# Short-sequence attention on one core: transposes straight from the landed tiles, v by four rows a partition

## The chip, the cores and the metric

One core of a Trainium2 chip. The metric is the device time of one execution in microseconds (us). Every run lists a span (first to last instruction) and the clock that TensorE was granted. The profile is one execution; the times come from several, and the span of a profiled run is about 1.8 us shorter than its time. Executions fall into a fast and a slow state (the changed kernel: 139.7 to 140.9 us fast, 142.3 us slow). The medians below are of all runs of a kernel, the ratios of its fast runs alone; where it matters, the fast runs are named.

Engines: PE is TensorE (PEld its weight loads), DVE is VectorE, ACT is ScalarE, POOL is GpSimd, SP is SyncE. "The DMA" is the core's 16 DMA engines; the profile's page gives its shares of the time of all 16. In quoted lines "<-" names what ended a wait: a tile that another engine wrote or freed, a landing (DMA), PE's own sequencer (PEq), or "issue" where the profile shows nothing that was waited for.

## The reference

```python
batch, n_heads, seq, head_dim = 32, 12, 128, 64          # q, k, v: f32, 12.6 MB each
scores = 1 / np.sqrt(64) * np.matmul(q, k.transpose(0, 1, 3, 2))
attn = np.exp(scores - np.max(scores, axis=-1, keepdims=True))
attn = attn / (np.sum(attn, axis=-1, keepdims=True) + 1e-8)
return np.matmul(attn, v)
```

There are 384 heads. 37.75 MB are read and 12.58 MB written; the arithmetic is small.

## The kernel before

The heads go in 48 units of 8, and four units make a super-tile. A slab is a piece of q, k, v or the output with so many consecutive rows in each of the 128 partitions. POOL loads q, k and v and casts them from f32 to bf16 on the way (37.75 MB read from HBM, 18.87 MB landed by the packet sizes of the trace). q and k land with 16 consecutive rows of a head in one partition. DVE pairs rows of two slabs (128 values side by side), PE transposes the pairs with an identity, DVE empties the transposes' one PSUM bank, and scores, exponential, values and normalisation follow. v's keys are brought into the same order by matmuls with a selection matrix.

```python
NQ, NVB, NVE, NP, NT, NA = 4, 2, 8, 4, 2, 4      # buffers: q and k each, v, ordered v, pairs, ...
q_b = [sb(f"q_b{i}", [128, 2, 16 * D], bf16) for i in range(NQ)]
v_b = [sb(f"v_b{i}", [128, 4, RV * D], bf16) for i in range(NVB)]      # RV = 8 rows a partition
...
def pair_up(t):                                    # DVE
    src = (q_b, k_b)[j][s % NQ][:].rearrange("p a (r d) -> p r a d", d=D)
    return nc.vector.tensor_copy(pair[t_index[t] % NP][:], src[:, 8 * b:8 * b + 8])
...
for u in steps:                                    # one step a unit; the order of every engine's list
    for t in t_at.get(u, []): pe_transposes(t)     # waits for the pair and for the bank being empty
    for m in v_at.get(u, []): pe_order_v(m); act_keep(m)
    pe_scores(u + 1); act_exps(u + 1); pe_values(u); dve_normalise(u - 1)
    for t in t_at.get(u, []): dve_keep(t)          # empties the bank
    for t in t_at.get(u + 2, []): dve_pair(t)      # two steps AHEAD of the transposes
...
# POOL's loads: q and k wait for the pairs made of the buffer's last tile,
# v waits for the order matmuls of the group two before
deps = [("P", t) for t in t_order if t[0] == x - NQ and t[1] == j]
deps = [("V", sum(vgroups[:x - NVB + 1]) - 1)]
```

PE's list is a loop over 8 steps (two super-tiles). Its instructions name fixed buffers, so of what PE reads for a super-tile there are no more than two buffers here, one for each super-tile of the loop. The pairing copies are unrolled on DVE; that is why q and k could have four.

The softmax here doesn't subtract the row's maximum and nothing guards it: scores larger than these inputs give would overflow.

Of the kernel before, what the change touches and what calls it, by code (L numbers as in the profile page):

```python
# [10 lines left out]
def kernel(  # L11
# [7 lines left out]
    nc = tc.nc  # L19
# [13 lines left out]
    RO, SO = 4, S // 4  # L33
    RV, SV = 8, S // 8
    supers, u0 = [], 0
# [10 lines left out]
    k_rows = {R: slabs(k, R) for R in (16,)}  # L46
    v_rows, o_rows = slabs(v, RV), slabs(out, RO)

# [9 lines left out]
    vgroups = [4] * (NU // 4)  # L58
    stores = [1, 1] + [2] * ((NU - 4) // 2) + [1, 1]
    assert sum(vgroups) == NU and sum(stores) == NU  # L60
# [17 lines left out]
    for m in range(NU):  # L78
        v_at[m - 3] = [m]
    steps = range(min(t_at) - 2, NU + 1)  # L80

    NQ, NVB, NVE, NP, NT, NA = 4, 2, 8, 4, 2, 4

# [13 lines left out]
    ident = sb("ident", [128, 128], bf16)  # L97
    sel = {R: sb(f"sel{R}", [128, 8, 2, 32], bf16) for R in (16,)}
    q_b = [sb(f"q_b{i}", [128, 2, 16 * D], bf16) for i in range(NQ)]
    k_b = [sb(f"k_b{i}", [128, 2, 16 * D], bf16) for i in range(NQ)]  # L100
    v_b = [sb(f"v_b{i}", [128, 4, RV * D], bf16) for i in range(NVB)]
    v_e = [sb(f"v_e{i}", [128, 8, D + 1], bf16) for i in range(NVE)]
    pair = [sb(f"pair{i}", [128, 8, 2, D], bf16) for i in range(NP)]
    qkT = [sb(f"qkT{i}", [128, 2, 16, S], bf16) for i in range(NT)]
# [64 lines left out]
    def transposes(t):  # L169

        s, j, b = t
        R = supers[s][0]
        x = pair[t_index[t] % NP]
        p = qk_ps[:].rearrange("p (h r j s) -> p h r j s", h=R, r=4, j=2)
        for r in range(8):
            jj, r4 = divmod(r, 4)
            i = nc.tensor.transpose(  # L177
                p[:, :, r4, jj, :], x[:, r].rearrange("p a d -> p (a d)"), ident[:])
        return i

    def order_v(m):


        g, w, n, first = vplace[m]
        pick = sel[supers[of_unit[first]][0]]
        nh = 8 // n
        t = v_ps[:].rearrange("p (i n e) -> p i n e", i=nh, e=D)
        for i in range(nh):
            for jv in range(2):
                for r4 in range(4):  # L190
                    x = nc.tensor.matmul(  # L191
                        t[r4 * 32:(r4 + 1) * 32, i, :, :],
                        lhsT=pick[:, w * nh + i, jv, :],
                        rhs=v_b[g % NVB][:, :n, (4 * jv + r4) * D:(4 * jv + r4 + 1) * D],
                        start=jv == 0, stop=jv == 1)
        return x

    def v_at_head(u, a, h):

        R, f = supers[of_unit[u]]  # L200
        g, _, n, first = vplace[u]
        n8, h8 = divmod(a * R + 4 * (u - f) + h, 8)
        if n == 2:
            n8 = a
        nh = 8 // n
        return first + h8 // nh, (h8 % nh) * n + n8

# [30 lines left out]
    def exps(u):  # L238
# [5 lines left out]
            func=EXP, bias=0.0, scale=scale)  # L244

    def pair_up(t):

        s, j, b = t
        src = (q_b, k_b)[j][s % NQ][:].rearrange("p a (r d) -> p r a d", d=D)
        return nc.vector.tensor_copy(pair[t_index[t] % NP][:], src[:, 8 * b:8 * b + 8])  # L250

# [40 lines left out]
    def pe_transposes(t):  # L292
        i = t_index[t]
        deps = [("P", t)] + ([("E", t_order[i - 1])] if i else [])
        op("PE", ("T", t), lambda: transposes(t), deps, ["pe_dve"])

    def pe_wait(kind, key):
# [34 lines left out]

    def dve_pair(t):
        s, j, b = t
        deps = [("T", t_order[t_index[t] - NP])] if t_index[t] >= NP else []
        dma = [((s_q, s_k)[j][s % NQ], 16 * (s // NQ + 1))]
        op("DVE", ("P", t), lambda: pair_up(t), deps, ["dve_io"] if t_index[t] else ["dve_pe", "dve_io"], dma)

    def dve_keep(t):
        s = t[0]  # L340
        deps = [("T", t)]
        for x in range(s):
            if x % NT == s % NT:
                R, f = supers[x]
                deps.append(("S", f + R // 4 - 1))
        op("DVE", ("E", t), lambda: keep_qk(t), deps, ["dve_pe"])

# [23 lines left out]
    def store(c):  # L371
# [17 lines left out]
        last = first + n - 1  # L389
        op(name, ("store", c), emit, [("N", last if c in own else max(last, HELD))])  # L390

    def pool_load(kind, x):
        deps = []
        if kind == "v":
            if x >= NVB:
                deps = [("V", sum(vgroups[:x - NVB + 1]) - 1)]
            n, first = vgroups[x], sum(vgroups[:x])
            op("POOL", ("load", kind, x), lambda: nc.gpsimd.dma_start(  # L398
                out=v_b[x % NVB][:, :n, :], in_=v_rows[:, first:first + n, :],
            ).then_inc(s_v[x % NVB], 16), deps)  # L400
            return
# [3 lines left out]
        if x >= NQ:  # L405
            deps = [("P", t) for t in t_order if t[0] == x - NQ and t[1] == j]
        n = f * 8 // R
# [6 lines left out]


    op("ACT", ("K", -1), lambda: nc.scalar.drain(), [], ["act_pe"], v_landing(0))
    at_step = {}
    for u in steps:
# [20 lines left out]
        for t in t_at.get(u, []):  # L439
            dve_keep(t)  # L440
        for t in t_at.get(u + 2, []):
            dve_pair(t)
        for o in program["PE"][start:]:
# [3 lines left out]
    for s in range(len(supers)):  # L447
        for j in range(2):
            loads.append((t_step[s, j, 0] - 2, "qk"[j], s))
    for g in range(len(vgroups)):  # L450
        m = sum(vgroups[:g])

        loads.append((vstep_of[m] - 1.5 + (2 if 2 <= g < len(vgroups) - 2 else 0), "v", g))
    loads.sort(key=lambda e: e[0])
# [9 lines left out]
    seen = {e: {} for e in program}  # L464
    waited_dma = {e: {} for e in program}

# [31 lines left out]
    def tensor_program():  # L498
# [11 lines left out]
        for place in [(l, kind) for l in range(PERIOD) for kind in "TVSOQ"]:  # L510
# [4 lines left out]
            skipped = 0 if trips[0] else TRIPS - 1  # L515
            if waiting or not places or places[-1][0] != skipped or place == (1, "T"):
                places.append((skipped, waits[place] if waiting else [], []))
# [5 lines left out]
        with nc.Fori(  # L523
                0, TRIPS, engines=bass.OrderedEngineSet([nc.tensor.engine]),
                head_slot={nc.tensor.engine: 128}):
            for skipped, always, some in places:
                run_waits("PE", always)
                with nc.tensor.If_ne(trip, skipped):
                    for o, w in some:
                        run("PE", o, w)  # L530
            nc.tensor.reg_add(trip, trip, 1)
# [19 lines left out]

    for t in sel.values():
        nc.vector.memset(t[:], 0.0)
    nc.vector.memset(ident[:], 0.0).then_inc(s_zero, 1)
# [3 lines left out]

    for jv in range(2):
        nc.vector.tensor_copy(  # L560
            sel[16][:].rearrange("p h v (x y s) -> p h v x y s", x=2, y=2)[:, :, jv, :, jv, :],
            ident[:].rearrange("p (h s x) -> p h x s", h=8, x=2))
    for o in program["DVE"]:
# [38 lines left out]
```

## Time and profile before

| | |
|---|---|
| time | 134.2 us, median of 3 (132.2 to 134.65); 133.8 with the fourth run |
| span of the profiled run | 131.9 us |
| DMA | full from the second slice of 40 to the third from the end |
| DVE, PE, ACT busy | 69%, 74%, 56% |

The DMA row is the only one that is full nearly everywhere. The lines and their reading stand in the prediction.

### The profile page before, as it was taken

To read this page: it belongs to the slowest core of one execution; us is meant where nothing else is said; L and a number is where in the kernel's file an instruction comes from. 1 tells how busy PE (TensorE), PEld (TensorE's weight loads), DVE (VectorE), ACT (ScalarE), POOL (GpSimd) and SP (SyncE) were. 2 spreads that over 40 slices of the span, in tenths; PEclk is the share of its full clock that TensorE was granted. 3 is DMA by queue.
4 is the path that set the end of the run, shared out by engine and by line. 5 is a ranking of instruction groups with operands and counts; after the bars stand their busy time and mean duration, and the time that the engine had idled before them with its cause. 6 is when DMAs were issued, how large, how long until landed. Compare 5 with 4: busy or idle time off the path is not lost. (4 is left out here: it accounts for less than half of the span.)

```text
span 131.9 us, 7079 instructions
## 1 busy us (share of the span) xinstructions
PE 97.0 (74%) x3072; PEld 68.9 (52%) x3072; DVE 90.8 (69%) x214; ACT 73.7 (56%) x97; POOL 55.5 (42%) x81
## 2 busy tenths in 40 slices
PE   0014989994989999869849839978669998877610
PEld 0013647672667677656627626656456766555410
DVE  1126366895588999969939848969826988875740
ACT  0000528845577778476367366498084868588700
POOL 5950005015008259194460391390680399930000
PEclk9999999999599999999999999999986999999955
DMA  2999999999999999999999999999999999999982
GB/s 15 164 206 210 208 208 213 209 207 212 204 213 165 167 222 237 209 327 251 208 318 259 209 279 217 212 353 220 212 348 225 211 342 270 400 380 368 319 289 82
DMA packets 18248, 31.56 MB, mean 239 GB/s; under 512 B 1344, under 2 KB 9536, under 8 KB 18240
## 3 DMA queue, kind: packets, MB, share of 16 engines
q0 software_dynamic: 16064, 29.36, 101.3%
q1 hardware_dynamic: 2176, 2.10, 4.7%
q8 instruction: 4, 0.07, 0.2%
q14 instruction: 4, 0.03, 0.1%
HBM read 37.75 MB, written 12.58 MB: 381 GB/s over the span
## 5 line engine op out<-in xcount | busy, mean ns | idle before, releaser
L241 ACT ACTIVATE attnT<-s_ps 128x1024 bf16<-128x1024 f32 x48 | 49.4, 1030 | 0.4 <-PE s_ps L217 0.4
L236 ACT CAST v_e<-v_ps 128x512 bf16<-128x512 f32 x48 | 28.2, 588 | 37.0 <-PE v_ps L191 19.1
L177 PE MATMUL qk_ps<-ident,pair 128*128 128x128 bf16 x384 | 32.2, 232 | 15.3 <-PEq L478 15.1
L191 PE MATMUL v_ps<-v_b,sel 128*32 128x256 bf16 x768 | 31.9, 289 | 11.3 <-PEq L478 11.2
L272 DVE TENSOR_TENSOR o_sb<-o_ps,recip 128x512 f32<-128x512 f32 (+1 forms) x53 | 34.0, 641 | 4.8
L259 DVE COPY qkT<-qk_ps 128x1024 bf16<-128x1024 bf16 x48 | 32.8, 684 | 5.3 <-PE qk_ps L177 4.3
L177 PEld LDWEIGHTS qk_ps<-ident,pair 128*128 128x128 bf16 x384 | 24.2, 103 | 20.4 <-issue 17.9
L398 POOL DMA_DIRECT2D v_b<-in_v_dram x12 | 9.5, 791 | 59.7 <-PE v_ps L191 59.7
L387 POOL DMA_DIRECT2D out_dram<-o_sb x38 | 27.2, 729 | 0.0
L191 PEld LDWEIGHTS v_ps<-v_b,sel 128*32 128x32 bf16 x768 | 16.9, 99 | 17.8 <-issue 13.6
L228 PE MATMUL o_ps<-v_e,attnT 128*32 128x65 bf16 x1536 | 22.6, 200 | 1.7 <-PEq L478 0.8
L269 DVE RECIPROCAL recip<-o_ps 128x8 f32<-128x8 f32 (+1 forms) x53 | 10.5, 198 | 16.8 <-PE o_ps L228 16.0
L228 PEld LDWEIGHTS o_ps<-v_e,attnT 128*32 128x32 bf16 x1536 | 16.7, 98 | 7.5 <-issue 3.8
L217 PE MATMUL s_ps<-qkT 64*128 64x128 bf16 x384 | 19.5, 222 | 0.7 <-PEq L478 0.6
L217 PEld LDWEIGHTS s_ps<-qkT 64*128 64x128 bf16 x384 | 11.1, 95 | 11.3 <-issue 11.3
L250 DVE COPY pair<-q_b 128x1024 bf16<-128x1024 bf16 x24 | 11.1, 460 | 6.3 <-DMA q_b<-in_q_dram 6.2
L250 DVE COPY pair<-k_b 128x1024 bf16<-128x1024 bf16 x24 | 10.2, 427 | 0.0
L410 POOL DMA_DIRECT2D q_b<-in_q_dram x12 | 9.0, 747 | 1.0 <-SPq L96 1.0
L236 ACT ACT_TABLE_LOAD x1 | 1.3, 1283 | 13.7 <-DMA v_b<-in_v_dram 13.7
L410 POOL DMA_DIRECT2D k_b<-in_k_dram x12 | 8.6, 721 | 0.0
L560 DVE COPY sel<-ident 128x128 bf16<-128x128 bf16 x2 | 0.4, 224 | 1.8 <-POOL ident L537 1.8
L384 POOL DMA_DIRECT2D out_dram<-o_sb x2 | 1.5, 734 | 0.0
(8 smaller groups left out, 1.4 us busy)
## 6 DMA issues: line engine op xcount, KB each, us to landing
out_dram<-o_sb POOLq DMA_DIRECT2D x40, 256.0 KB, 10.2
q_b<-in_q_dram POOLq DMA_DIRECT2D x12, 512.0 KB, 13.2
k_b<-in_k_dram POOLq DMA_DIRECT2D x12, 512.0 KB, 12.7
v_b<-in_v_dram POOLq DMA_DIRECT2D x12, 512.0 KB, 10.2
out_dram<-o_sb SPq DMA_DIRECT2D x8, 256.0 KB, 4.3
```

The source lines that it names most:

```text
L177: i = nc.tensor.transpose(p[:, :, r4, jj, :], x[:, r].rearrange("p a d -> p (a d)"), ident[:])
L191: x = nc.tensor.matmul(t[r4 * 32:(r4 + 1) * 32, i, :, :], lhsT=pick[:, w * nh + i, jv, :], rhs=v_b[g % NVB][:, :n, (4 * jv + r4) * D:(4 * ...
L217: i = nc.tensor.matmul(t[:, a, h, :], lhsT=x[p, 1, 4 * w + h, :], rhs=x[p, 0, 4 * w + h, :], start=True, stop=True)
L228: y = nc.tensor.matmul(t[h * SO:(h + 1) * SO, a, r * (D + 1):(r + 1) * (D + 1)], lhsT=x[:, a, h, r * SO:(r + 1) * SO], rhs=v_e[m % NVE][:, ...
L236: return nc.scalar.copy(v_e[m % NVE][:, :, :D], v_ps[:].rearrange("p (n e) -> p n e", e=D))
L241: return nc.scalar.activation(out=attnT[u % NA][:].rearrange("p a h (r s j) -> p (a h r) s j", r=4, j=J), in_=s_ps[u % 2][:].rearrange("p ...
L250: return nc.vector.tensor_copy(pair[t_index[t] % NP][:], src[:, 8 * b:8 * b + 8])
L259: return nc.vector.tensor_copy(x.rearrange("p h (r j s) -> p (h r) j s", r=4, j=J)[:, :, 2 * b:2 * b + 2, :].rearrange("p x j s -> p x (j ...
L269: nc.vector.reciprocal(r, o4[:, :, :, D]).then_inc(s_r, 1)
L272: return nc.vector.tensor_mul(o[:, :, w, :].rearrange("p a (r d) -> p a r d", d=D), o4[:, :, :, :D], r.unsqueeze(3).to_broadcast([128, o4. ...
L387: e.dma_start(out=dst[:, a], in_=src[:, a]).then_inc(s_o[lane(c)], 16)
L410: nc.gpsimd.dma_start(out=bufs[x % NQ][:], in_=rows[R][:, n:n + 2, :]).then_inc(sm[x % NQ], 16)
```

## The change

Its intent is to drop 21 us of DVE copies and a third of the order matmuls' busy time on PE. Transposes read the landed q and k tiles, two of 64 columns where there was one of 128. v lands with 4 rows in a partition, eight slabs a group, so that one selection matrix of 32 columns puts its keys in order with 4 matmuls of 512 columns. q and k have two buffers, since PE reads them itself now. The kernel gives PE no wait for a transfer in its loop, so DVE waits for the next landing before it empties the bank.

```diff
-    v_rows, o_rows = slabs(v, RV), slabs(out, RO)
+    v_rows, o_rows = slabs(v, RO), slabs(out, RO)
-    stores = [1, 1] + [2] * ((NU - 4) // 2) + [1, 1]
+    stores = [1, 1] + [2] * ((NU - 8) // 2) + [1] * 6
-        v_at[m - 3] = [m]
+        v_at[m - 4] = [m]
-    NQ, NVB, NVE, NP, NT, NA = 4, 2, 8, 4, 2, 4
+    NQ, NVB, NVE, NT, NA = 2, 2, 8, 2, 4
 ...
-        x = pair[t_index[t] % NP]
+        x = (q_b, k_b)[j][s % NQ][:].rearrange("p a (r d) -> p r a d", d=D)[:, 8 * b:8 * b + 8]
         for r in range(8):
             jj, r4 = divmod(r, 4)
-            i = nc.tensor.transpose(
-                p[:, :, r4, jj, :], x[:, r].rearrange("p a d -> p (a d)"), ident[:])
+            for a in range(2):
+                i = nc.tensor.transpose(
+                    p[a * D:(a + 1) * D, :, r4, jj, :], x[:, r, a], ident[:])
 ...
-        for i in range(nh):
-            for jv in range(2):
-                for r4 in range(4):
-                    ...  # 16 matmuls of 256 columns, two accumulating
+        for r4 in range(4):
+            x = nc.tensor.matmul(
+                t[r4 * 32:(r4 + 1) * 32], lhsT=sel[:, w, :],
+                rhs=v_b[g % NVB][:, :, r4 * D:(r4 + 1) * D], start=True, stop=True)
 ...
-        op("DVE", ("E", t), lambda: keep_qk(t), deps, ["dve_pe"])
+        op("DVE", ("E", t), lambda: keep_qk(t), deps, ["dve_pe"], qk_landing(t_index[t] + 1))
 ...
-            deps = [("P", t) for t in t_order if t[0] == x - NQ and t[1] == j]
+            deps = [("T", t) for t in t_order if t[0] == x - NQ and t[1] == j]
 ...
-        for t in t_at.get(u + 2, []):
-            dve_pair(t)
 ...
-            loads.append((t_step[s, j, 0] - 2, "qk"[j], s))
+            loads.append((t_step[s, j, 0], "qk"[j], s))
-        loads.append((vstep_of[m] - 1.5 + (2 if 2 <= g < len(vgroups) - 2 else 0), "v", g))
+        loads.append((vstep_of[m], "v", g))
```

(Cut: the removed pairing, the selection matrix, which stores wait for which mark, and the slot of PE's loop head, `head_slot`, 128 to 132.)

More of the change, by code (lines that the diff above doesn't have):

```diff
@@ L33 @@
     RO, SO = 4, S // 4
-    RV, SV = 8, S // 8
     supers, u0 = [], 0
@@ L78 @@
     for m in range(NU):
-        v_at[m - 3] = [m]
-    steps = range(min(t_at) - 2, NU + 1)
-    NQ, NVB, NVE, NP, NT, NA = 4, 2, 8, 4, 2, 4
+        v_at[m - 4] = [m]
+    steps = range(min(t_at), NU + 1)
+    NQ, NVB, NVE, NT, NA = 2, 2, 8, 2, 4
     MIXED, OWN, HELD = 24, 40, NU - 8
@@ L97 @@
     ident = sb("ident", [128, 128], bf16)
-    sel = {R: sb(f"sel{R}", [128, 8, 2, 32], bf16) for R in (16,)}
+    sel = sb("sel", [128, 4, 32], bf16)
     q_b = [sb(f"q_b{i}", [128, 2, 16 * D], bf16) for i in range(NQ)]
     k_b = [sb(f"k_b{i}", [128, 2, 16 * D], bf16) for i in range(NQ)]
-    v_b = [sb(f"v_b{i}", [128, 4, RV * D], bf16) for i in range(NVB)]
+    v_b = [sb(f"v_b{i}", [128, 8, RO * D], bf16) for i in range(NVB)]
     v_e = [sb(f"v_e{i}", [128, 8, D + 1], bf16) for i in range(NVE)]
-    pair = [sb(f"pair{i}", [128, 8, 2, D], bf16) for i in range(NP)]
     qkT = [sb(f"qkT{i}", [128, 2, 16, S], bf16) for i in range(NT)]
@@ L184, in order_v @@
         g, w, n, first = vplace[m]
-        pick = sel[supers[of_unit[first]][0]]
-        nh = 8 // n
-        t = v_ps[:].rearrange("p (i n e) -> p i n e", i=nh, e=D)
-        for i in range(nh):
-            for jv in range(2):
-                for r4 in range(4):
-                    x = nc.tensor.matmul(
-                        t[r4 * 32:(r4 + 1) * 32, i, :, :],
-                        lhsT=pick[:, w * nh + i, jv, :],
-                        rhs=v_b[g % NVB][:, :n, (4 * jv + r4) * D:(4 * jv + r4 + 1) * D],
-                        start=jv == 0, stop=jv == 1)
+        t = v_ps[:].rearrange("p (n e) -> p n e", e=D)
+        for r4 in range(4):
+            x = nc.tensor.matmul(
+                t[r4 * 32:(r4 + 1) * 32], lhsT=sel[:, w, :],
+                rhs=v_b[g % NVB][:, :, r4 * D:(r4 + 1) * D], start=True, stop=True)
         return x
     def v_at_head(u, a, h):
-        R, f = supers[of_unit[u]]
-        g, _, n, first = vplace[u]
-        n8, h8 = divmod(a * R + 4 * (u - f) + h, 8)
-        if n == 2:
-            n8 = a
-        nh = 8 // n
-        return first + h8 // nh, (h8 % nh) * n + n8
+        g, w, n, first = vplace[u]
+        return first + h, 4 * a + w
     def scores(u):
@@ L244, in exps @@
             func=EXP, bias=0.0, scale=scale)
-    def pair_up(t):
-        s, j, b = t
-        src = (q_b, k_b)[j][s % NQ][:].rearrange("p a (r d) -> p r a d", d=D)
-        return nc.vector.tensor_copy(pair[t_index[t] % NP][:], src[:, 8 * b:8 * b + 8])
     def keep_qk(t):
@@ L293, in pe_transposes, with qk_landing @@
         i = t_index[t]
-        deps = [("P", t)] + ([("E", t_order[i - 1])] if i else [])
+        deps = [("E", t_order[i - 1])] if i else [("I", 0)]
         op("PE", ("T", t), lambda: transposes(t), deps, ["pe_dve"])
+    def qk_landing(i):
+        s, j, b = t_order[i] if i < len(t_order) else (0, 0, 1)
+        return [] if b else [((s_q, s_k)[j][s % NQ], 16 * (s // NQ + 1))]
     def pe_wait(kind, key):
@@ L331, in act_exps @@
         op("ACT", ("X", u), lambda: exps(u), deps, ["act_pe"])
-    def dve_pair(t):
-        s, j, b = t
-        deps = [("T", t_order[t_index[t] - NP])] if t_index[t] >= NP else []
-        dma = [((s_q, s_k)[j][s % NQ], 16 * (s // NQ + 1))]
-        op("DVE", ("P", t), lambda: pair_up(t), deps, ["dve_io"] if t_index[t] else ["dve_pe", "dve_io"], dma)
     def dve_keep(t):
@@ L389, in store @@
         last = first + n - 1
-        op(name, ("store", c), emit, [("N", last if c in own else max(last, HELD))])
+        if c not in own:
+            last = max(last, HELD)
+        heard = last + 8 <= t_step[t_order[-1]]
+        op(name, ("store", c), emit, [("Q", last + 1) if heard else ("N", last)])
     def pool_load(kind, x):
@@ L398, in pool_load @@
             op("POOL", ("load", kind, x), lambda: nc.gpsimd.dma_start(
-                out=v_b[x % NVB][:, :n, :], in_=v_rows[:, first:first + n, :],
+                out=v_b[x % NVB][:], in_=v_rows[:, 2 * first:2 * (first + n), :],
             ).then_inc(s_v[x % NVB], 16), deps)
@@ L413, in pool_load @@
         op("POOL", ("load", kind, x), emit, deps)
+    op("DVE", ("I", 0), lambda: nc.vector.drain(), [], ["dve_pe"], qk_landing(0))
     op("ACT", ("K", -1), lambda: nc.scalar.drain(), [], ["act_pe"], v_landing(0))
@@ L464 @@
     seen = {e: {} for e in program}
-    waited_dma = {e: {} for e in program}
     def waits_of(engine, o):
@@ L515, in tensor_program @@
             skipped = 0 if trips[0] else TRIPS - 1
-            if waiting or not places or places[-1][0] != skipped or place == (1, "T"):
+            if waiting or not places or places[-1][0] != skipped or place == (2, "T"):
                 places.append((skipped, waits[place] if waiting else [], []))
@@ L524, in tensor_program @@
                 0, TRIPS, engines=bass.OrderedEngineSet([nc.tensor.engine]),
-                head_slot={nc.tensor.engine: 128}):
+                head_slot={nc.tensor.engine: 132}):
             for skipped, always, some in places:
@@ L549 @@
         run("ACT", o, waits_of("ACT", o))
-    for t in sel.values():
-        nc.vector.memset(t[:], 0.0)
     nc.vector.memset(ident[:], 0.0).then_inc(s_zero, 1)
@@ L557 @@
     nc.vector.wait_ge(s_id, 1)
-    for jv in range(2):
-        nc.vector.tensor_copy(
-            sel[16][:].rearrange("p h v (x y s) -> p h v x y s", x=2, y=2)[:, :, jv, :, jv, :],
-            ident[:].rearrange("p (h s x) -> p h x s", h=8, x=2))
+    nc.vector.tensor_copy(
+        sel[:].rearrange("p h (j s) -> p h j s", j=4),
+        ident[:].rearrange("p (h s j) -> p h j s", h=4, j=4))
     for o in program["DVE"]:
```

## The prediction

> **What bounds the kernel now.** I read the slices of the span first, to see whether any one row is full from end to end.
>
> ```profile
> PE   0014989994989999869849839978669998877610
> DVE  1126366895588999969939848969826988875740
> DMA  2999999999999999999999999999999999999982
> GB/s 15 164 206 210 208 208 213 209 207 212 204 213 165 167 222 237 209 327 251 208 318 259 209 279 217 212 353 220 212 348 225 211 342 270 400 380 368 319 289 82
> ```
>
> Only the DMA row is full, from the third slice to the third from the end. GB/s counts bytes as they land, and loads land as bf16 while they are read as f32; so 210 GB/s in the slices that only load is about 420 GB/s read from HBM. Next, the bytes and the busy shares:
>
> ```profile
> PE 97.0 (74%) x3072; PEld 68.9 (52%) x3072; DVE 90.8 (69%) x214; ACT 73.7 (56%) x97; POOL 55.5 (42%) x81
> ...
> q0 software_dynamic: 16064, 29.36, 101.3%
> ...
> HBM read 37.75 MB, written 12.58 MB: 381 GB/s over the span
> ```
>
> 50.3 MB at about 415 GB/s is 121 us of the 131.9 us span. The chain that ended last holds only 3% DVE and 1% PE: it covers the last 6 us and doesn't explain the span. So I asked for the transfers in two stretches of 5 us: 21.5 to 26.5 us (almost only q and k) and 26.5 to 31.5 us (q, k and v).
>
> ```profile
> DMA packets 554, 1.05 MB, mean 209 GB/s; under 512 B 33, under 2 KB 53, under 8 KB 554
> ```
>
> and the second:
>
> ```profile
> DMA packets 784, 1.04 MB, mean 208 GB/s; under 512 B 30, under 2 KB 522, under 8 KB 784
> ```
>
> One row of q or k in a partition is 16x64 values: 4096 B read, a packet of 2048 B landed. One of v is 8x64: 2048 B read, 1024 B landed. Packets under 512 B are semaphores. The first stretch has 501 q/k and about 20 v packets in 5 us x 16 engines = 80,000 engine-ns: about 156 ns per q/k packet. The second has 262 q/k and 492 v: (80,000 - 262x156)/492 = about 80 ns per v packet. (The recorded packet times, 173 and 98 ns in the trace, overlap; that is why the share exceeds 100%.) Halving the read bytes thus saves 76 ns of 156, and a fixed 4 ns a packet remains.
>
> Then the places where that flow is not full. Windows: the stretch 40 to 48.5 us, and the end.
>
> ```profile
> 22.00:40.00 18.00, 15.45 (x478) 10.97 (x477) 13.94 (x31) 11.37 (x16) 3.63 (x5) 0.91 1.15 209
> 40.00:48.50 8.50, 8.32 (x302) 6.06 (x299) 7.74 (x19) 6.97 (x10) 4.29 (x6) 1.00 1.02 164
> 48.50:114.00 65.50, 53.88 (x1794) 38.58 (x1792) 51.30 (x112) 41.31 (x56) 37.15 (x53) 0.97 1.13 264
> 114.00:132.00 18.00, 9.01 (x351) 6.21 (x348) 9.58 (x28) 9.28 (x12) 2.57 (x4) 0.81 0.83 295
> ```
>
> (Columns: length; busy time and count of PE, PEld, DVE, ACT, POOL; clock; DMA share; GB/s.) From 40 to 48.5 us loads flow at 164 instead of 209: 22% of 8.5 us = 1.9 us of transfer time lost, with PE busy 98%. The cause shows in the waits: POOL issues all loads in order and sat before the loads of v until the second-last group of v had been put in order.
>
> ```profile
> POOL v_b L398 <- PE v_ps L191: 59.7, 10, 12.8
> ```
>
> In the timeline of POOL the v load at 40.23 us came 8.75 us after the previous issue; by then only about 3 MB, 7 to 8 us of work, had been queued. In the other 65 us to 114 the engines keep waiting for data instead (ACT waits 17.8 us for v landings): compute has slack. The last v lands at 113.4 us by the packet records, the last normalisation ends at 126.9, the last store packet at 130.15; stores stay short of the full rate by about 2 us between 114 and 130.
>
> [...]
>
> **The change part by part.**
>
> *Pairing copies removed (DVE).* 24x460 + 24x427 ns = 21.3 us of 90.8. In the middle DVE's step is then 0.20 (reciprocal) + 0.69 (multiply) + 0.68 (copy of q/k) = 1.57 us, with gaps about 1.7, against about 2.05. Beside the DMA: worth nothing by itself, except where compute holds back loads.
>
> *Transposes from the landed tiles.* 384 of 128x128 become 768 of 128x64 with 128 moving columns, in two column groups. If pairs overlap, [...]about 0.62 us a step as now. Zero.
>
> *v put in order by 4 matmuls of 512 columns instead of 16 of 256.* [...]0.62 to about 0.40 us a step, 48 times, 10.6 us of PE time, hidden as well.
>
> *v in rows of 4.* 6144 packets of 2048 B read become 12,288 of 1024 B. By the packet costs above: 768 per engine x 42 ns = 32.3 us instead of 384 x 80 = 30.7: +1.6 us; a fit over all 5 us stretches (155 and 81) gives 44 ns and +2.7. I take **+2.0 us, on the path**, because the DMA is the bound.
>
> *Order and depth of loads.* q and k go from 4 buffers to 2; the order becomes q, v, k, each issued when the transposes (or orders) of two super-tiles earlier are done. When PE waits for q of the next super-tile, its v and k and the following q are queued: 3 MB, over 7 us, and the next load is issued about 1 us after that landing. So I expect no hole. The load-only stretch needs 3 MB per 4 steps, 7.4 us or 1.86 us a step; the old step of 1.85 to 2.2 us couldn't hold that, the new one of about 1.75 just can. **-1.9 us**: the hole at 40 us goes.
>
> *The end.* 20 units of stores instead of 24 go ahead of the last load, six single-unit stores replace pairs, and steps 41 to 48 get shorter (13.5 us now, I estimate 11 to 12). So the transfers, not compute, set the end. Of the 2 us of shortfall I count half: **-1.0 us**.
>
> *Sum.* +2.0 - 1.9 - 1.0 = -0.9 us. The span goes from 131.9 to about 131.0; the profiled run took 133.7 us for its 131.9 us span, so about 132.8 us, and I shade it to 132.6 because the v cost may be hidden by the same overlap that hides most of today's per-packet time. Against the median of 134.2 that is 1.2% less; against the profiled run, 0.8%.
>
> **Rivals.**
> *A: the 512 B landings are dearer than a straight line says.* At the recorded, unoverlapped time (173, 98, so about 60 ns) v would cost 46 us instead of 30.7: about 148 us. Against: packets overlap throughout the loading stages, and 1024 B store packets took 47 ns on the SP queue. A milder form (48 ns) gives +6 us, about 137.
> *B: compute becomes the bound in the load-only stretch.* If the 64-column transposes don't run in pairs, they take [...]over 1.0 us, and the step 2.2 us; over some 18 steps that is 0.3x18 = 5 us of hole: about 138. DVE now also waits for the next landing before it empties the transposes, which couples the engines closer to arrivals. For: single qk_ps bank. Against: the overlap seen in the v matmuls. [...]
> *C: the step speed matters more than I say.* If hole and shortfall go entirely and the v rows cost nothing: -3.9 us, about 129.8.
>
> **Range and chances.** The terms are each good to 1 or 2 us, and timed runs of before already spread from 132.2 to 134.65. C needs two favourable terms together for over 2% (below 131.5); A or B in mild form gives over 2% slower. Range 129.8 to 135.8; faster 0.29, same 0.58, slower 0.13.
>
> **What would show it.** DMA row full from 5 us to the last two slices and no dip in GB/s near slice 12; 12,288 more or less packets of 512 B with recorded times of about 60 ns (98 now); HBM read in loading slices at 405 to 412 instead of 415 to 420 GB/s; transposes at about 0.62 us a step and the order at 0.40; POOL's wait for the order matmuls no longer followed by a hole. Wrong if v packets record 70 ns or more (A), if transposes take 1 us a step at full clock, if the clock is at half for many slices (B), or if the DMA row shows holes that start after a POOL wait on transposes: then two q/k buffers were too few.

## The result

140.4 us (139.7 to 142.3, 4 runs) against 133.8 us (132.2 to 134.65, 4 runs): **slower**, ratio 1.0554, 95% interval 1.0388 to 1.0721. A ratio here is the mean time of one kernel's fast runs over that of the other's fast runs of the same rounds, so not quite the ratio of the medians quoted. The fast runs behind the ratio are three of 139.7 to 140.9 us against two, 132.2 and 133.45 us. The prediction said 132.6 us, in a range of 129.8 to 135.8.

The busy times and slices of the changed kernel, and its packet count:

```profile
PE 91.8 (66%) x2880; PEld 62.4 (45%) x2880; DVE 75.0 (54%) x164; ACT 73.7 (53%) x97; POOL 57.5 (42%) x81
...
PE   0052739999859998589977667686839856857200
...
DVE  1020322788835888356857547684744844877600
...
GB/s 11 174 203 211 200 212 72 133 210 178 184 194 201 209 146 150 276 202 235 336 197 236 333 200 246 247 204 327 238 196 326 242 206 338 401 389 361 338 327 51
DMA packets 24392, 31.56 MB, mean 228 GB/s; under 512 B 1344, under 2 KB 15680, under 8 KB 24384
```

The dip of the kernel before, at its 13th and 14th slices (165 and 167), is not at that place (201 and 209), but there is a deeper one at the seventh and eighth (72 and 133) and another at the fifteenth and sixteenth (146 and 150). A slice is 3.45 us. There are 6144 packets more, as the v rows demand.

The groups of the parts that the change made cheaper or dearer (busy us and mean ns, then idle time before):

```profile
L383 POOL DMA_DIRECT2D v_b<-in_v_dram x12 | 10.9, 904 | 57.6 <-PE v_ps L186 54.0
L176 PE MATMUL qk_ps<-ident,q_b 128*64 128x128 bf16 x384 | 18.4, 247 | 20.6 <-PEq L460 18.1
...
L186 PE MATMUL v_ps<-v_b,sel 128*32 128x512 bf16 x192 | 21.1, 430 | 1.7 <-ACT attnT L229 0.9
```

The kernel before had:

```profile
L191 PE MATMUL v_ps<-v_b,sel 128*32 128x256 bf16 x768 | 31.9, 289 | 11.3 <-PEq L478 11.2
```

Order matmuls take 21.1 us of PE instead of 31.9. The pairing copies, 21.3 us, are gone; DVE's busy time falls by less, from 90.8 to 75.0 us, since the groups of the kernel before overlap (they add up to over 98 us). The work on the engines that was to go is gone, and the kernel is slower.

Two stretches of the windows (length, then PE, PEld, DVE, ACT, POOL busy, clock, DMA share, GB/s):

```profile
20.00:26.00 6.00, 5.15 (x108) 3.26 (x110) 2.05 (x4) 3.06 (x4) 2.31 (x3) 1.00 0.63 90
...
48.00:56.00 8.00, 7.28 (x264) 5.13 (x260) 6.77 (x14) 6.34 (x9) 4.77 (x7) 1.00 1.12 154
```

In both, loads alone are in flight, and 90 and 154 GB/s land where about 205 could (the slices just before the first stretch have 203, 211, 200 and 212). The DMA's *share* in the second is 1.12 as in a full stretch: packets are in progress, only they take longer (the longest q/k packet there took 1.17 us instead of 0.17). So the share alone doesn't show such a hole; the GB/s do.

What POOL's issues look like at the start, in the timeline of POOL (start, duration, what, in brackets the idle time before and what ended it):

```profile
10.83 0.72 POOL L395 DMA_DIRECT2D q_b<-in_q_dram  x1 [4.24 <-PE qk_ps L176]
22.67 0.89 POOL L383 DMA_DIRECT2D v_b<-in_v_dram  x1 [11.13 <-PE v_ps L186]
23.56 0.71 POOL L395 DMA_DIRECT2D k_b<-in_k_dram  x1
```

Six loads go out in the first 6.6 us (not shown), the seventh at 10.8, and the eighth only at 22.7. Seven loads of 1 MB each at about 415 GB/s (twice the 200 to 212 that land in the slices above, bf16 for f32), from 3.05 us on, would be done by about 21 us; in the packet records nearly all of them have ended at 22.0 us, and a few packets follow until 23.2. So the queue ran dry. The eighth load's first packet starts at 24.27 us, 1.6 us after its issue, and it landed at 28.8.

Why it took until 22.7 shows in the timeline of the same kernel between 13 and 23 us:

```profile
13.56 0.69 DVE L241 COPY qkT<-qk_ps 128x1024 bf16<-128x1024 bf16 x1 [4.25 <-DMA k_b<-in_k_dram]
...
14.40 1.22 PE L176 MATMUL qk_ps<-ident,k_b 128*64 128x128 bf16 x16 [3.33 <-PEq L460]
...
16.49 1.06 PE L176 MATMUL qk_ps<-ident,k_b 128*64 128x128 bf16 x16 [0.33 <-PEq L460]
...
18.43 0.32 PE L176 MATMUL qk_ps<-ident,q_b 128*64 128x128 bf16 x2 [0.33 <-PEq L460]
...
20.85 0.96 PE L176 MATMUL qk_ps<-ident,q_b 128*64 128x128 bf16 x14 [2.10 <-issue]
...
21.74 0.62 PE L186 MATMUL v_ps<-v_b,sel 128*32 128x512 bf16 x4
```

The load of v waits for the last order matmul of v's first group, at 21.74. In PE's list that stands behind the first transposes of the *next* q, those behind DVE's copy of the last k, and that behind the landing of k at 13.5. So three rounds of transposes and copies at about 2 us each (sixteen transposes take 1.06 us here and 0.64 later) lie between that landing and the release, and a stall of 2.1 us in the midst of sixteen transposes. An instruction packet of 16 KB is read from 18.41 to 19.30; the stall begins at 18.75 and lasts to 20.85. The next q itself had landed at 15.85, before the copy at 17.59 that waits for it: the landing that counts here is the one of k, and what follows it is the engines' own chain.

**How the holes were measured.** In a stretch I count the packets that ended and weigh them with their cost in full stretches, in engine-ns: 155 for q/k, 81 for 1024 B of v, 44 for 512 B of v, 159 for a 4096 B store, 47 for a 1024 B store. The sum over 16 engines, taken from the stretch's length, is the hole. The packets under 512 B are left out: 1344 of 4 bytes in each of the two profiles, 16 for each of the 84 transfers issued, as many as the kernel's semaphores count for one. Values within a few tenths of zero are the error of those costs.

| us of hole | 4 to 60 us | 60 to 112 us | 112 us to the last packet |
|---|---|---|---|
| before | 2.2 | -0.2 | 2.1 |
| changed | 6.1 | -0.6 | 2.1 |

The last packet moved from 130.15 to 136.26 us, 6.1 us. Holes account for 3.5 of that, and v's packets, 768x44 - 384x81 ns, for 2.7.

### The profile page after: what moved, and what is told of

Its sections match the earlier page's. It is cut to its first block, busy times and chain, and to the rows that moved or that the text cites. A ratio compares the mean times of both kernels' runs of the same rounds, so it can differ in the third digit from the quotient of the medians.

```text
span 138.1 us, 6648 instructions
## 1 busy us (share of the span) xinstructions
PE 91.8 (66%) x2880; PEld 62.4 (45%) x2880; DVE 75.0 (54%) x164; ACT 73.7 (53%) x97; POOL 57.5 (42%) x81
## 2 busy tenths in 40 slices
DMA packets 24392, 31.56 MB, mean 228 GB/s; under 512 B 1344, under 2 KB 15680, under 8 KB 24384
## 5 line engine op out<-in xcount | busy, mean ns | idle before, releaser
L383 POOL DMA_DIRECT2D v_b<-in_v_dram x12 | 10.9, 904 | 57.6 <-PE v_ps L186 54.0
L176 PE MATMUL qk_ps<-ident,q_b 128*64 128x128 bf16 x384 | 18.4, 247 | 20.6 <-PEq L460 18.1
L176 PE MATMUL qk_ps<-ident,k_b 128*64 128x128 bf16 x384 | 17.8, 242 | 11.7 <-PEq L460 10.9
L176 PEld LDWEIGHTS qk_ps<-ident,q_b 128*64 128x64 bf16 x384 | 14.5, 125 | 23.5 <-issue 23.1
L216 PE MATMUL o_ps<-v_e,attnT 128*32 128x65 bf16 x1536 | 23.3, 201 | 2.7 <-PEq L460 2.5
L186 PE MATMUL v_ps<-v_b,sel 128*32 128x512 bf16 x192 | 21.1, 430 | 1.7 <-ACT attnT L229 0.9
L216 PEld LDWEIGHTS o_ps<-v_e,attnT 128*32 128x32 bf16 x1536 | 17.2, 99 | 8.9 <-issue 5.2
L205 PE MATMUL s_ps<-qkT 64*128 64x128 bf16 x384 | 20.3, 229 | 0.9 <-PEq L460 0.6
L176 PEld LDWEIGHTS qk_ps<-ident,k_b 128*64 128x64 bf16 x384 | 14.1, 123 | 14.7 <-issue 13.9
L186 PEld LDWEIGHTS v_ps<-v_b,sel 128*32 128x32 bf16 x192 | 5.0, 94 | 7.1 <-issue 4.0
```

Source lines behind the costliest of these rows:

```text
L176: i = nc.tensor.transpose(p[a * D:(a + 1) * D, :, r4, jj, :], x[:, r, a], ident[:])
L186: x = nc.tensor.matmul(t[r4 * 32:(r4 + 1) * 32], lhsT=sel[:, w, :], rhs=v_b[g % NVB][:, :, r4 * D:(r4 + 1) * D], start=True, stop=True)
L205: i = nc.tensor.matmul(t[:, a, h, :], lhsT=x[p, 1, 4 * w + h, :], rhs=x[p, 0, 4 * w + h, :], start=True, stop=True)
L216: y = nc.tensor.matmul(t[h * SO:(h + 1) * SO, a, r * (D + 1):(r + 1) * (D + 1)], lhsT=x[:, a, h, r * SO:(r + 1) * SO], rhs=v_e[m % NVE][:, ...
L383: op("POOL", ("load", kind, x), lambda: nc.gpsimd.dma_start(out=v_b[x % NVB][:], in_=v_rows[:, 2 * first:2 * (first + n), :],).then_inc(s_ ...
```

## The experiments

Times are medians of all runs; "before" ran beside each batch at 132.4 to 132.7 us. The changed kernel was not run again in these batches.

### A longer loop on PE, and deeper buffers

```diff
-    PERIOD, FIRST = 8, -8
+    PERIOD, FIRST = 16, -16
```

> A control: the changed kernel with TensorE's loop over 16 steps instead of 8, which is what other buffer counts need, and nothing else. Theory H (the loss is holes in the load stream, because q and k have only two buffers) and rival V (the loss is dearer v packets) both expect the changed kernel's time, about 140.4 us, ratio to before 1.045 to 1.065, with a hole in GB/s near 21 to 27 us. If the startup stall of 2.1 us inside TensorE's transposes at 18.7 us is instruction fetch, a longer loop body may move it and change the time by up to 2 us.

Measured: 188.6 us, ratio 1.42 (the profiled span is 187.0 us instead of 138.1). A surprise, and it's good that the control was run. In the page's queue of instruction fetches there are 33 packets instead of 4:

```profile
q8 instruction: 33, 0.54, 1.3%
```

PE sat idle before its transposes, with nothing but "issue" as the reason, for 39.6 us, against 2.1 us in the changed kernel. The 33 packets are spread from 2.6 to 182 us; the four of the changed kernel all start by 22.1 us. From these times I infer that the loop of 16 steps was fetched again and again, the one of 8 only in its first pass.

```diff
-    NQ, NVB, NVE, NT, NA = 2, 2, 8, 2, 4
+    NQ, NVB, NVE, NT, NA = 4, 4, 8, 2, 4      # on top of the loop of 16 steps
```

> The same loop of 16 steps with four buffers each for q, k and v. H: the three holes (3.3, 0.9 and 1.9 us of transfer time by the packet records of the changed kernel) go, so 140.4 - 6.1 = about 134.3 us, ratio to before 1.00 to 1.015. V: the packets are as small as before, so it stays above 138 us, ratio above 1.03.

Measured: 181.1 us, ratio 1.37. The time says nothing on the question, since PE's waits with nothing but "issue" as the reason, 33.7 us here before the transposes, weigh on both kernels. What can be read is the start: with deep buffers there is no hole up to 72 us, where p16 has one of 5.5 us between 20 and 30 us. It is consistent with short queues as the cause, and no more.

### v by eight rows again, without pairing

```diff
-    v_rows = slabs(v, RO)                     # 4 rows, 4 matmuls of 512 columns
+    v_rows = slabs(v, RV)                     # 8 rows, 16 matmuls of 256 columns, as before
```

(In short: the selection matrix and the 16 matmuls come back with it, word for word as before.)

> The changed kernel with v loaded again by 8 rows a partition (2048 B read, 1024 B landed) and put in order by 16 matmuls of 256 columns as before; no pairing, two buffers. H: only the packet cost comes back, 768x44 - 384x81 ns = 2.7 us, so about 137.9 us, ratio 1.03. V: nearly all of it comes back, 135 us or less, ratio below 1.015.

Measured: 140.2 us, ratio 1.0495 (1.041 to 1.058). Both theories missed: the packets are the cheap ones again and nothing came back. Its holes from 4 to 60 us are 8.6 us instead of 6.1: what the packets gave, the holes took. (A later expectation says 8.3, by an earlier count.) TensorE waits at the start for 1.9 us and 2.7 us with no data missing, where a 16 KB instruction packet had just started each time. So the packets alone aren't the loss.

### Two buffers in the kernel before

```diff
-    NQ, NVB, NVE, NP, NT, NA = 4, 2, 8, 4, 2, 4
+    NQ, NVB, NVE, NP, NT, NA = 2, 2, 8, 4, 2, 4
```

> The kernel before with two buffers instead of four for q and for k, all else (pairing, v by 8 rows, order of loads) as it was. H: shallow loads alone make holes, 2 to 5 us more, ratio 1.015 to 1.04. V: no change, ratio within 1 per cent of 1.

Measured: 132.4 us, ratio 1.001 (0.992 to 1.010). My theory H in that form fell: two buffers alone make no hole. Here they even left none at 40 us:

```profile
GB/s 13 173 198 210 212 207 212 212 205 212 205 213 204 209 288 204 219 360 198 212 364 197 211 288 207 222 356 201 216 356 213 212 356 273 405 396 354 304 316 43
```

Holes from 4 to 60 us: 0.4 us instead of 2.2. Yet the time is the same, so the hole that I read in one profile of the kernel before wasn't worth 1.9 us of its median.

The theory that replaced it (H2): the pairing copies let a buffer go as soon as it landed, two steps ahead of the transposes; without them q, k and v all come free only where PE has got to.

### The v part alone

The kernel before, with v by 4 rows and 4 order matmuls, each one step earlier:

```diff
-    v_rows, o_rows = slabs(v, RV), slabs(out, RO)
+    v_rows, o_rows = slabs(v, RO), slabs(out, RO)
-        v_at[m - 3] = [m]
+        v_at[m - 4] = [m]
```

(Cut: the selection matrix and the order matmuls, as in the change.)

> The kernel before with only the v part of the change: rows of 4, 4 matmuls of 512 columns a step, each order one step earlier (it has to be, a group of v now serves all four units); pairing, four buffers of q and k and the order of loads stay. Theory H2 (the loss is holes, and they come from taking the pairing away; packets cost 2.0 to 2.7 us): about 135 us, ratio 1.015 to 1.025, the DMA row full. Rival V (the v packets carry the loss, hidden in the v8 run by something else): 138 us or more, ratio above 1.04. Rival N (packets cost nothing on the path): ratio within 0.7 per cent of 1.

Measured: 135.1 us, ratio 1.0165 (1.010 to 1.023), 2.4 us more than before, and no hole up to 60 us (1.8 us between 60 and 112). The dearer packets are real and of the size that the prediction gave them.

### Pairing one step ahead instead of two

```diff
-        for t in t_at.get(u, []):
-            dve_keep(t)
-        for t in t_at.get(u + 2, []):
+        for t in t_at.get(u + 1, []):
             dve_pair(t)
+        for t in t_at.get(u, []):
+            dve_keep(t)
```

> The kernel before with two buffers of q and k, and the pairing copies made one step ahead of the transposes instead of two: copies, packets and matmuls are all as before, only q and k come free later and DVE meets the landings later. H2: part of the holes of the changed kernel appear, 134 to 137 us, ratio 1.01 to 1.035. Rival F (the holes come from instruction fetch in TensorE's longer list of transposes): no change, ratio within 1 per cent of 1.

Measured (on top of two buffers): 134.4 us, ratio 1.0151 (1.008 to 1.023). Nothing but the look-ahead differs from b_nq2, whose interval in its own batch was 0.992 to 1.010, and the matmuls are the same in both, so rival F doesn't explain the difference. It supports H2. The holes between 4 and 112 us rise from 0.7 to 2.3 us, but that proves little: the profile of the kernel before, with the full look-ahead, has 2.0 us, and both have theirs mainly between 40 and 48 us.

### The order of loads

```diff
-        loads.append((vstep_of[m], "v", g))
+        loads.append((vstep_of[m] + 1.5, "v", g))
```

> The changed kernel with its loads issued in the order q, k, v instead of q, v, k. The third load of k is then not behind the load of v that waits for TensorE. H2: 1 MB more is queued before the hole at 21 us, so up to 2.5 us of 3.3 us goes: 137.5 to 138.5 us, ratio 1.035 to 1.045. Rival F or V: 140 us still.

Measured: 138.8 us, of four runs between 137.3 and 142.3. Two of the four are of the slow state, so there is no verdict; the two fast ones took 137.28 and 137.32. Its profiled run (137.3 us) has 3.7 us of holes up to 60 us instead of 6.1. The direction is as H2 said.

### Order matmuls ahead of transposes

```diff
+        for m in v_at.get(u, []):
+            pe_order_v(m)
+            act_keep(m)
         for t in t_at.get(u, []):
             pe_transposes(t)
-        for m in v_at.get(u, []):
-            pe_order_v(m)
-            act_keep(m)
```

(Cut: the same exchange in the list from which PE's loop is built, and PE's last waits.)

> The changed kernel with the order matmuls ahead of the transposes in each step of TensorE's list, so that v comes free without waiting for the landing of the next q. H2: the third v load goes out about 2 to 3 us earlier, the hole near 21 us shrinks from 3.3 to about 1 us and those near 36 and 50 us shrink too: 136 to 138 us, ratio 1.02 to 1.04. Rivals: 140 us.

Measured: 136.2 us, ratio 1.0296 (1.021 to 1.038): 4.2 us less than the changed kernel by the medians, 3.7 by the means of the fast runs, 2.6% by the ratios (the two intervals, 1.021 to 1.038 and 1.039 to 1.072, just don't overlap). The third v load, expected 2 to 3 us earlier, goes out 1.7 us earlier, and later ones up to 4.3 us (43.30 instead of 47.64):

```profile
20.96 0.89 POOL L383 DMA_DIRECT2D v_b<-in_v_dram  x1 [7.29 <-PE v_ps L186]
```

The same two stretches:

```profile
20.00:26.00 6.00, 5.95 (x114) 3.79 (x113) 2.38 (x5) 3.68 (x5) 2.30 (x3) 1.00 1.03 146
...
48.00:56.00 8.00, 7.05 (x256) 4.96 (x251) 6.43 (x14) 6.02 (x8) 4.65 (x7) 1.00 1.20 241
```

146 instead of 90 GB/s, 241 instead of 154 (some of the latter are stores, which by then have begun earlier). Holes up to 60 us: 1.8 us. No engine's work changed and no transfer either; only the place of the order matmuls in PE's list, and so the moment at which v's buffer comes free, did. PE's stall of 2.1 us isn't gone either: there is one of 2.5 us in this run, still ahead of the third v load. This is the clearest proof that the late release of v's buffer, behind the next q's transposes, was a loss. It doesn't show that q's landing was what held those transposes; the experiment on DVE's wait, below, speaks against it.

### Both mends

The v8 kernel with the order matmuls first.

> The changed kernel with both mends: v by 8 rows again and the order matmuls ahead of the transposes. The v8 run alone gained nothing although its packets cost 2.5 us less, because its holes grew from 6.1 to 8.3 us. If packets and holes add up (H2), both mends give 136.2 - 2.5 = 133.7 us, ratio 1.00 to 1.015. If v by 8 rows brings its own loss whatever the holes (rival W), it stays at 136 us or more.

Measured: 138.6 us, ratio 1.0379. The sum of 133.7 isn't reached; rival W's number is nearer. (Against v8, 140.2 us, the order of PE's list gains 1.2 to 1.6 us by the fast runs here too, less than with 4 rows.) Holes up to 60 us are 6.8 us; PE stalls for 3.1 us after 14.8 us and 2.1 us after 22.0 us. The second run of the same kernel, with no edit (its label speaks of a slot, but it has none):

> Placeholder for the same kernel as v8_vfirst, run again: 138.6 us within 1 us, stalls of 3.1 and 2.1 us of TensorE after 14.8 and 22.0 us again, if they come from the fetch of instructions and not by chance.

Measured: 138.8 us, ratio 1.0459. Stalls of 3.9 and 1.5 us at the same two order matmuls. Their place isn't chance; their size varies.

### Where the head of PE's loop lies

Rival F is that PE's stalls, which lie near fetches of instruction packets, are the loss. On the changed kernel it is the stall of 2.1 us from 18.75 us, beside the packet of 18.41 to 19.30 us. By an instruction block the expectations mean one of those packets of 16 KB; that `head_slot` counts places in it is the author's reading, which no run shows by itself.

```diff
-                head_slot={nc.tensor.engine: 132}):
+                head_slot={nc.tensor.engine: 64}):
```

On the changed kernel:

> The changed kernel with the head of TensorE's loop at another place of an instruction block (64 instead of 132)[...]. If that stall is what delays the third v load (rival F in its mild form), the hole at 21 us shrinks by about 2 us: 138.3 us, ratio 1.04. If it's only incidental, 140.4 us within 1 us; the stall then shows at another line.

Measured: 138.8 us, ratio 1.042 (1.031 to 1.053); the profiled run is of the slow state. The third v load does go out at 20.3 instead of 22.7 us, and the stall shows a step later. The hole between 20 and 30 us is 1.1 us instead of 3.3, as rival F in its mild form expected, though others make up for it in that slow run. Its three fast runs, 137.8 to 138.8 us, lie under the changed kernel's 139.7 to 140.9; but the interval overlaps that of the changed kernel (1.039 to 1.072), which ran in another batch. So a gain of 1 to 2 us is likely and not established: part of the first hole may be the stall's.

On v8_vfirst:

> The v8_vfirst kernel with TensorE's loop head at slot 64 of an instruction block instead of 132. If its two stalls (3.1 us after 14.8 us, 2.1 us after 22.0 us) are instruction fetches on the way to the loads, they move; 135 to 137.5 us if they fall into waits for data, 138.6 if they only fall elsewhere on the path. If rival W holds (v by 8 rows brings a loss of its own) the stalls stay at the same matmuls.

Measured: 139.8 us, ratio 1.054. The stalls moved (2.6 us ahead of 16.8 us, 1.6 us after 20.6 us), the time didn't fall.

On a_vfirst:

> The a_vfirst kernel with the loop head at slot 64. Its stall of 2.5 us inside the order matmul at 17.5 us moves away; the third v load goes out before 19.5 us instead of at 21.0 and the hole of 1.6 us near 22 us shrinks below 0.8 us: 135.2 to 136 us, ratio 1.02. If the stall has nothing to do with fetch, it stays at the order matmul and the time at 136.2 us.

Measured: 137.8 us, ratio 1.038 (1.031 to 1.044). The stall moved as expected. In a_vfirst it was inside the four matmuls of one order step:

```profile
20.05 0.61 PE L186 MATMUL v_ps<-v_b,sel 128*32 128x512 bf16 x2 [2.51 <-issue]
```

With the other slot it is ahead of another:

```profile
22.94 0.62 PE L186 MATMUL v_ps<-v_b,sel 128*32 128x512 bf16 x4 [1.42 <-PEq L460]
```

But the time rose, and the hole near 22 us shrank only to 1.1 us while others grew to 1.8. So the stalls are tied to a place in the instruction list, as they would be if they came from the fetches; that is inferred from their places (1.4 to 3.9 us each in these runs) and no more. Moving the loop only moves them, and it paid in none of three kernels beyond doubt. That they matter when they fall on the way to a release is likely, not shown.

### DVE's wait for the next landing

```diff
-        op("DVE", ("E", t), lambda: keep_qk(t), deps, ["dve_pe"], qk_landing(t_index[t] + 1))
+        op("DVE", ("E", t), lambda: keep_qk(t), deps, ["dve_pe"])
+        op("DVE", ("L", t), lambda: nc.vector.drain(), [], ["dve_pe"], qk_landing(t_index[t] + 1))
```

(Cut: PE's next transposes wait for L where they waited for E.)

On top of a_vfirst.

> The run with the order matmuls first, with DVE's wait for the next landing moved behind the copy out of the transposes' bank, as an operation of its own. If that wait held the scores back (a part of H2), 0.5 to 1.5 us less than 136.2; otherwise the same within 0.7 us, since the transfers set the pace.

Measured: 136.3 us, ratio 1.0282, a_vfirst had 136.2. That coupling costs nothing by itself.

### The pairing, at equal packets, buffers and order

```diff
-    NQ, NVB, NVE, NP, NT, NA = 4, 2, 8, 4, 2, 4      # on top of b_v4
+    NQ, NVB, NVE, NP, NT, NA = 2, 2, 8, 4, 2, 4
```

> The b_v4 kernel with two buffers of q and k instead of four. Against a_qkv (138.8 us) it has the same v packets, the same buffers and the same order q, k, v of the loads; the difference is mainly the pairing copies two steps ahead. If the pairing is what kept the stream full: 135 us within 0.8, ratio 1.01 to 1.025. If it was the four buffers: 137.5 us or more, ratio above 1.035.

Measured: 135.2 us, ratio 1.0213 (1.014 to 1.028), all four runs fast. The 138.8 us of a_qkv hold two slow runs; against its fast ones, 137.3 us, the difference is 2.1 us. POOL's loads after the first six, with pairing (b_v4_nq2):

```profile
8.20 0.72 POOL L399 DMA_DIRECT2D q_b<-in_q_dram  x1 [1.61 <-DVE pair L239]
15.34 0.71 POOL L399 DMA_DIRECT2D k_b<-in_k_dram  x1 [6.42 <-DVE pair L239]
20.50 0.89 POOL L387 DMA_DIRECT2D v_b<-in_v_dram  x1 [4.45 <-PE v_ps L187]
```

and without (a_qkv):

```profile
11.01 0.70 POOL L395 DMA_DIRECT2D q_b<-in_q_dram  x1 [4.44 <-PE qk_ps L176]
17.80 0.71 POOL L395 DMA_DIRECT2D k_b<-in_k_dram  x1 [6.09 <-PE qk_ps L176]
23.45 0.87 POOL L383 DMA_DIRECT2D v_b<-in_v_dram  x1 [4.94 <-PE v_ps L186]
```

Each load goes out 2.5 to 3 us earlier with the pairing, released by DVE's copy for q and k instead of PE's transposes. There is no hole up to 60 us with it and 3.7 us without; between 60 and 112 us it is the other way, 1.5 us with and none without, so 2.0 us remain, about the difference in time. The two kernels also differ in the last stores, in the order of the first six loads, and in PE's list, which has 8 transposes a step with pairing and 16 without, and another slot of the loop head. So this pair doesn't exclude rival F; the pair b_nq2 and b_nq2_la1 does for the look-ahead.

### An attempt at something better

```diff
-    MIXED, OWN, HELD = 24, 40, NU - 8
+    MIXED, OWN, HELD = 24, 48, NU - 8      # on top of b_nq2: POOL issues all stores
```

> An attempt at something better than both: the kernel before with two buffers of q and k, and all stores issued by POOL, also the last eight units that SP issued. POOL's stores land in packets of 4096 B at 159 ns, SP's in 1024 B at 47 ns or more when mixed; the end is short of the full rate by 2.1 to 2.6 us in all runs. If those small packets are the cause, 1 to 1.5 us less than before, ratio 0.988 to 0.993; if the end waits for compute instead, no gain, ratio 0.997 to 1.01.

Measured: 135.4 us, ratio 1.0218 (1.016 to 1.028). Worse: the last packet ends at 129.5 us, but the span ends 3.3 us later instead of 1.8, and this profile has a hole of 1.5 us at 40 us again. No kernel of the study beats the one before; b_nq2 equals it with half the q and k buffers.

## Why the prediction was wrong

**What held.** The DMA bounds the kernel, and engine time saved beside it bought nothing. Transposes in two column groups do run in pairs: sixteen in 0.64 us, predicted 0.62, where eight of 128 columns took 0.61 before. In the trace a pair of them starts every 56 ns, as one did before. Order matmuls take 0.40 us a step, as the author had estimated; before, sixteen took 0.62, in fours that start within 10 ns of each other and about 100 ns after the last four. The v packets record 60 ns, as the straight line through 173 and 98 said, and the v part alone costs 2.4 us where the prediction took 2.0: rival A is refuted.

**The step that failed** is "So I expect no hole", in "Order and depth of loads", with its ground: "the next load is issued about 1 us after that landing". The next q landed at 15.8 us and the v load that was to follow went out at 22.67, 6.9 us later; at the landing of q at 43.3 us it was 4.3 us. The prediction looked at what is *queued* when PE waits, and left out the chain between a landing and the release: DVE's copies, three rounds of transposes through one bank (counted from k's landing at 13.5 us), and the order matmul at their end, with PE's slow rounds at the start and its stall of 2.1 us. And POOL issues in order, so the k that was already free stood behind the v that wasn't (23.56 after 22.67 us). The "-1.9 us" thus became +3.5 us of holes between the two profiles. a_vfirst shows it by taking most of the holes away with a reordered list (1.8 us of 6.1 remain up to 60 us). b_nq2, b_nq2_la1 and b_v4_nq2 against a_qkv point to what had prevented it: the pairing copies were a look-ahead of two steps. I had called them "worth nothing by itself, except where compute holds back loads", and did not follow that exception. The prediction's own sign, "POOL's wait for the order matmuls no longer followed by a hole", failed at 22.7 us. Its warning that "two q/k buffers were too few" isn't shown: the hole follows a wait for v's order matmuls and not for transposes, and b_nq2, with pairing, has two and no loss. Deeper buffers without pairing were tried in p16deep alone, whose time says nothing.

**The hole at 40 us** of the kernel before was there (1.9 us) but read wrongly in part, and valued wrongly. "Only about 3 MB" seems to count the last three loads before POOL's wait; by the landings five were unfinished then, at 31.5 us, and two still at 40.23, the last landing at 43.6. So POOL's wait alone doesn't explain it. b_nq2 has no such hole and isn't faster by its median.

**The end**, "-1.0 us", didn't come: 2.1 us of shortfall in both.

**Rival B** came nearest in size (about 138 us) with the wrong cause, since the transposes do run in pairs. The clock did fall in places: the trace has it at 0.5 from 41.49 to 44.90 us, beginning in a wait of 1.0 us, and from 58.55 us on, in a wait of 1.7 us; at 41.7 and at 59 us sixteen transposes take 1.06 us instead of 0.64. The kernel before has such a stretch from 32.94 to 36.35 us, after a wait of 1.9 us. Up to 24 us sixteen transposes take 1.06 us too (1.22 once); the clock row reads full speed there, but the trace has no clock record before 24.4 us. That the waits are the cause is not shown. **Rival A's** sum has a slip: 15.4 us more for v (46.1 instead of 30.7), on the base that gave 137 us for the milder form, make about 146 us, not 148.

By the ratios: 1.0554 in all; the v part alone 1.0165; with the order matmuls first 1.0296. As an estimate from these, about 2.6% was the late release of v, about 1.7% the packets, and some 1% is not accounted for: the profiles of a_vfirst and of b_v4 have the same holes after 4 us (3.7 and 3.8 us). The split isn't additive either, since putting the cheaper packets back (v8, v8_vfirst) gave nothing.

**What stays open.** How much of the hole at 22 us is PE's stall of 2.1 us; on the changed kernel moving it took 2.3 us of that hole away (in a profile of the slow state), and gained nothing certain in time. Why v by 8 rows without pairing (v8, v8_vfirst) has such large holes; its stalls are longer, but moving them didn't help. And why packets lengthen to about 1 us while the queue is short, though some are still queued: seen, not explained.

## What to carry to other kernels

In a kernel bound by transfers, a copy that costs an idle engine 21 us can be worth its time if it frees the landing buffer early (2.1 us in b_v4_nq2 against a_qkv, with the other differences named there): before removing it, follow the chain from a landing to the *next issue into that buffer*, in every engine's order, and compare that length with what is queued. In an in-order list, put the operation that frees a buffer ahead of operations that wait for new data (a_vfirst: 4.2 us less by the medians). And check the size of a loop body on PE before unrolling it further: with 16 steps for 8 it took 188.6 us instead of 140.4, with 33 instruction packets of 16 KB instead of 4.
